# Twenty-four weight slots instead of twenty-two, four experts of layer 0 with fixed tiles, ranking beside the first tile, another order of tiles

## The chip, the cores and the metric

The kernel runs on one core of one Trainium2 chip. The metric is device time in microseconds (us) of one launch; less is better. Engines are named as in the profile: PE is TensorE, DVE is VectorE, ACT is ScalarE, POOL is GpSimd, and SP is SyncE, which here issues all transfers. PEld is the loading of PE's stationary operand, and a q behind an engine's name is its sequencer.

## The reference

A two-layer transformer over 256 latent and 256 context tokens, width 1024, in float32. Layer 0 mixes tokens with windowed attention and latent attention, layer 1 with differential attention. After each mixer stands a mixture of experts: every token picks one of 4 groups and in it 2 of 8 experts, 32 experts in all. Layer 0 routes 512 tokens (1024 assignments), layer 1 only the 256 latent ones (512).

```python
g_logits = h @ w_group + b_group                 # 4 groups
grp = argmax(g_logits); p_grp = softmax(g_logits)[grp]
e_logits = (h @ w_expert + b_expert)[grp]        # 8 experts of that group
top_p, top_i = top_k(softmax(e_logits), 2)
gate = p_grp * top_p / sum(top_p); eid = grp * 8 + top_i
y = sum over the 2 experts: gate * ((silu(x @ w1[e]) * (x @ w3[e])) @ w2[e])
x = x + mod * y
```

One expert has w1 and w3 of 1024 x 512 and w2 of 512 x 1024, 6 MB in float32. Both layers together read 64 experts, 384 half matrices of 1 MB.

## The kernel before

**Slots.** Weights and large activations live in one pool of `NS` = 22 slots of 128 partitions x 2048 floats (1 MB, line 48; the pool is made at line 123). `S` takes one, `free(n)` gives back n data slots and `freew(n)` n weight slots. All weight loads stand in one list in the order of use (`plan`); `pump` emits them, in the order of the program, while the weight slots in use are fewer than `NS - max(budget, data slots in use, ...)`. `budget(n)` sets how many slots are kept for data. A load waits on the chip until the last reader of its slot is done. SP issues them in list order.

**Experts.** For each layer the planner sorts experts by how many tokens they have, and rank decides the room: `_tiles` packs the rooms of ranks into tiles of 128 rows. Kind A is one expert of 128 rows, B two (96 and 32), C two of 64, D three (64, 32, 32), E four of 32. The first `NFIX[l]` experts are not ranked: they have 64 rows each and fixed tiles (called F below), so their weights can be loaded before routing is known. Before the change layer 0 has one such tile and then C E B C E A B C E D B C; layer 1 has two and then E C E B E C E C E. Both changed and unchanged orders have 13 tiles in layer 0.

A tile's loads, in order: w1 (two halves of each of its experts), w3, w2. So A has 6 loads, B and C 12, D 18, E 24. Per tile PE makes ffn1 for w1 (L1334), combines the tile before it (L1381), makes ffn1 for w3, transposes, then ffn2 with w2 (L1364). After each half of a product `freew` frees its slots. Behind every second tile (and behind the first) the tokens of the next pair of tiles are gathered (L1317).

**Ranking.** `rank(l)` (L1164, DVE) turns the counts into a permutation of ranks. `rank_ids` (L1187) makes expert numbers of it with two small matmuls (L1191) and two DVE copies (L1192, L1193), and lifts the limit: loads of ranked experts read their expert number into a register (L213), and `limits` holds `pump` back to the loads of fixed experts until then. `rank` runs in the last step of `ffn_in`; `rank_ids` stands in `group_gather(0)`, between the gather of the first tile (L1276, copies at L1302) and its transposes (L1308, copies at L1309), ahead of the first expert matmul.

**Around it.** Before the last tile `rest` (L1384) stands: a loop over blocks of 64 tokens of experts that have more tokens than room, behind a branch (L1394). `budget(4 - l + 2 nh)` rules the tiles: 8 in layer 0, 5 in layer 1; for the last two tiles it is 14 and 12. Ahead of tile 0 the budgets are 8 and 5 too.

Of the kernel before, what the change touches and what calls it, by code (L numbers as in the profile page):

```python
# [10 lines left out]
F32 = mybir.dt.float32  # L11
F32R = mybir.dt.float32r
BF = mybir.dt.bfloat16
# [6 lines left out]
P = 128  # L20
# [24 lines left out]
    CN[_n] = (_o, _o + _w)  # L45
    _o += _w
NCN = _o
NS = 22
KU = 2

ADL = 3
# [3 lines left out]

NFIX = (2, 4)


def _tiles(nf, rooms, order):

    fix = [[(r, 64), (r + 1, 64)] for r in range(0, nf, 2)]
    left = {}
    for n, r in enumerate(range(nf, NE)):
        left.setdefault(rooms[n] if n < len(rooms) else 32, []).append(r)

    kinds = {"A": (128,), "B": (96, 32), "C": (64, 64), "D": (64, 32, 32), "E": (32,) * 4}
    tiles = []
    for k in order:  # L70
        t = []
        for n, w in enumerate(kinds[k]):
            t.append((left[w].pop(0 if n % 2 == 0 else -1), w))
        tiles.append(t)
    assert not any(left.values())
    return fix + tiles


TILES = [_tiles(2, (128,) + (96,) * 3 + (64,) * 9, "CEBCEABCEDBC"), _tiles(4, (96,) + (64,) * 6, "ECEBECECE")]
NTS = [len(ts) for ts in TILES]  # L80
COLS = [[rw_ for t in ts for rw_ in t] for ts in TILES]
assert all(all(sum(w for _, w in t) == P for t in ts) for ts in TILES)
# [34 lines left out]
def model_kernel(ctx: ExitStack, tc: tile.TileContext, xin, small, cst, ada0, adaw, win, wuq, wukv, wout0, dwin,  # L117
                 wout1, ew, out):
    nc = tc.nc
    PE, ACT, DVE, GP, SP = nc.tensor, nc.scalar, nc.vector, nc.gpsimd, nc.sync  # L120
    PSUM = bass.MemoryType.PSUM
    cp = ctx.enter_context(tc.tile_pool(name="cp", bufs=1))
# [22 lines left out]
    def freew(n):  # L145
        st_["w"] -= n
        pump()
# [50 lines left out]
    cs = {}  # L198
# [77 lines left out]
    cnE = cp.tile([P, 2, NE], F32, name="cnE")  # L276
    ones2 = cp.tile([P, 2], F32, name="ones2")
    DVE.memset(ones2, 1.0 / D)
    onesM = cp.tile([P, P], F32, name="onesM")
    DVE.memset(onesM, 1.0)  # L280
    epst = cp.tile([P, 2], F32, name="epst")
    DVE.memset(epst[:, 0:1], EPS)
    DVE.memset(epst[:, 1:2], DEPS)
    identB = cp.tile([P, P], BF, name="identB")
    maskB = cp.tile([P, 2, P], BF, name="maskB")
    UB = cp.tile([P, P], BF, name="UB")
    onesB = cp.tile([P, P], BF, name="onesB")
    DVE.memset(onesB, 1.0)
# [755 lines left out]
    def ffn_in(h, torder):  # L1044
# [89 lines left out]
            for t in range(2):  # L1134
                h_lo(t, 0, ((GP, DVE))[t])
        yield
        if last:
            rank(l)
            yield

        TT(pe, e4, b8(m4), ALU.subtract)
        TT(gx, g, b4(gmax), ALU.subtract)
# [21 lines left out]
    def rank(l):  # L1164

        key, tmp, st = U((NE,)), U((NE,)), T((4,))
        kc, rk, cc = (st[0:64, n:n + 1] for n in range(3))
        key, tmp = key[0:64], tmp[0:64]
        perm, tm2 = U((64,)), U((NE,))[0:64]
        GP.memset(perm[0:64], 0.0)  # L1170
        DVE.scalar_tensor_tensor(out=key, in0=cnts[0:64], scalar=32.0, in1=byl("tie", l)[0:64], op0=ALU.mult, op1=ALU.add)
        TT(tmp, key, ident[0:64, 0:NE], ALU.mult)
        TT(tm2, key, ident[0:64, NE:64], ALU.mult)
        TT(tmp, tmp, tm2, ALU.add)
        RD(out=kc, in_=tmp, axis=AX.X, op=ALU.add)
        DVE.tensor_scalar(tmp, key, kc, None, op0=ALU.is_gt)
        RD(out=rk, in_=tmp, axis=AX.X, op=ALU.add)
        for q in range(2):
            r = slice(32 * q, 32 * q + 32)
            DVE.tensor_scalar(perm[r, r], byl("rkc", l)[r], rk[r], None, op0=ALU.is_equal)  # L1180
            if q == 0:
                DVE.tensor_scalar(cc, kc, byl("tiec", l)[0:64], 1.0 / 32, op0=ALU.subtract, op1=ALU.mult)
        perm_[0], perm_[1] = perm, cc
# [95 lines left out]
    def moe(l, T_, gens, pre=None, hook=None):  # L1279
# [1 line left out]
        nh = nt // SEQ  # L1281
        cs_ = lambda c: slice(c * P, (c + 1) * P)

        def group_gather(g, mid=None):

            xg = S((KC, 256))
            oh = oh_of(g, T_)
            n = P * len(GROUPS[l][g])
            if n == P:
                xts = []  # L1290
                pss = pre if g == 0 and pre else [psA(), psA()]
                if g == 0:
                    gather0(T_, (0, 1), pss, 4 if pre else 0)
                for hf in range(2):
                    ps = pss[hf]
                    if g:
                        for t in range(T_):
                            for a, src in enumerate((hi_c, lo_c)):
                                PE.matmul(ps, oh[:, t, 0:n], src(t, slice(hf * 512, (hf + 1) * 512)),
                                          start=(t == 0 and a == 0), stop=(t == T_ - 1 and a == 1))  # L1300
                    xts.append(U())
                    (ACT.copy, DVE.tensor_copy)[hf](xts[hf], ps)  # L1302
                if mid:
                    mid()
                for hf in range(2):
                    ps = psB()
                    for q in range(4):
                        PE.transpose(ps[:, cs_(q)], xts[hf][:, cs_(q)], ident)  # L1308
                    (ACT.copy, DVE.tensor_copy)[hf](xg.v[:, 4 * hf:4 * hf + 4, 0:n],  # L1309
                                                    ps.rearrange("p (c n) -> p c n", c=4))  # L1310
                return xg
            for c0 in range(0, KC, 2):
                ps = psB()
                for i in range(2):
                    for t in range(T_):
                        for a, src in enumerate((hi_c, lo_c)):
                            PE.matmul(ps[:, i * n:(i + 1) * n], src(t, cs_(c0 + i)), oh[:, t, 0:n],  # L1317
                                      start=(t == 0 and a == 0), stop=(t == T_ - 1 and a == 1))
                ACT.copy(xg.v[:, c0:c0 + 2, 0:n], ps[:, 0:2 * n].rearrange("p (c n) -> p c n", c=2))
            return xg  # L1320
# [6 lines left out]
                return wts[key].rearrange("p (k n) -> p k n", k=4)  # L1327
            return f

        def ffn1(ps, parts, m, xg, ns):  # L1330
            for hf in range(2):
                for k in range(4):
                    for sl, wt in parts:
                        PE.matmul(ps[sl, :], xg(hf * 4 + k, sl), wt(m, hf)[:, k, :], start=(hf == 0 and k == 0),  # L1334
                                  stop=(hf == 1 and k == 3))
                freew(ns)

        def hmid_of(hm, p1, p3, sl=None):
            sl = U() if sl is None else sl
# [128 lines left out]
            free(4)  # L1468

        pend = None  # L1470
        xg_g = group_gather(0, rank_ids)
        for gen in gens:
            for _ in gen:
                pass
# [2 lines left out]
        for p in range(NT):  # L1477
# [16 lines left out]
            pm = []  # L1494
            for m in range(2):
                pm.append(psA())
                ffn1(pm[m], parts, m, xgc, len(segs))
                if m == 0:
                    sl = U()
                    ACT.activation(sl, pm[0], AF.Silu)  # L1500
                else:
                    hm = U()
                    TT(hm, sl, pm[1], ALU.mult)  # L1503
                if pend is not None:
                    combine(m, pend[0][m], pend[1], range(2 if m and p == NT - 1 else 4))
                elif p == 0 and m == 0:
                    pt = permute_t(T_)
                elif p == 0:
                    permute(T_, pt)
# [76 lines left out]
    fill(3)  # L1586
    next(last)
    fill(KC - ADL - 3)
    next(last)
    finish = moe(0, 4, (last, gen), pre, fill_all)  # L1590


# [235 lines left out]
    budget(5)  # L1828
    last = ffn_in(half, [0, 1])
    fillq.extend([(1, -5, k) for k in range(4)])  # L1830
    for n in (0, 0, 4, 0, 0):
        next(last)
        fill(n)
    finish = moe(1, 2, (last,), None, fill_all)
# [156 lines left out]
```

## Time and profile before

| | us |
|---|---|
| median of 3 runs | 1509.83 |
| lowest and highest | 1509.78, 1511.85 |
| profiled execution | 1511.53 |
| its span, first to last instruction | 1509.6 |

| engine | busy us | share of the span |
|---|---|---|
| PE | 1308.4 | 87% |
| PEld | 720.0 | 48% |
| DVE | 609.6 | 40% |
| ACT | 381.8 | 25% |
| POOL | 125.8 | 8% |

All transfers together are 487.07 MB, 323 GB/s over the span. A share over the whole span mixes stages: two attention blocks and two expert phases follow each other, and each has its own limit. The table to read is therefore one of stages, and then the waits in each.

### The profile page before, as it was taken

The page shows a single profiled execution, that of the slowest core. Times are in us where ns is not written, and L with a number is a line of the kernel's source. Part 1 is how long each engine was busy: PE and PEld are TensorE (multiplying, and loading weights), DVE is VectorE, ACT ScalarE, POOL GpSimd, SP SyncE. Part 2 cuts the span into 40 slices and gives each one's busy share as a digit, 9 for nine tenths or more (in the row PEclk, how much of TensorE's full clock was granted, in tenths as well). Part 3 has the DMA queues.
Part 4 walks back from the last instruction along what each step waited for, and adds up shares of the span by engine and source line. Part 5 has one row for each costly group of instructions (what it writes and reads, how often), then busy time and mean ns, then how long its engine had stood idle before and what let it go on. Part 6 is the DMA issues. An engine that isn't in the chain of part 4 may idle for free. (4 is left out here: it accounts for less than half of the span.)

```text
span 1509.6 us, 21525 instructions
## 1 busy us (share of the span) xinstructions
PE 1308.4 (87%) x8297; PEld 720.0 (48%) x8297; DVE 609.6 (40%) x1495; ACT 381.8 (25%) x814; POOL 125.8 (8%) x109
## 2 busy tenths in 40 slices
PE   6996989989999789987998999887998786887865
PEld 4673668945435235422435897584432221323322
DVE  4588895464222222221328657945311110111113
ACT  4445655331111001110115434642110100101002
POOL 1134011210000000000004211311000000000000
PEclk9998999999999999999999999999999999999997
DMA  9525624379999999999996227466999999999993
GB/s 381 214 97 197 222 91 162 140 296 388 402 420 421 421 421 413 383 395 422 420 419 273 84 84 294 156 236 283 420 421 421 421 421 420 421 420 422 419 408 154
DMA packets 68635, 487.07 MB, mean 323 GB/s; under 512 B 7472, under 2 KB 7600, under 8 KB 10928
## 3 DMA queue, kind: packets, MB, share of 16 engines
q1 hardware_dynamic: 68528, 485.64, 79.2%
q8 instruction: 67, 1.10, 0.3%
q14 instruction: 40, 0.33, 0.1%
HBM read 484.57 MB, written 1.05 MB: 322 GB/s over the span
## 5 line engine op out<-in xcount | busy, mean ns | idle before, releaser
L1334 PE MATMUL psA<-s 128*32 128x512 f32 (+2 forms) x2336 | 418.8, 618 | 90.0 <-DMA s<-in_ew_dram 84.7
L1334 PEld LDWEIGHTS psA<-s 128*32 128x32 f32 (+2 forms) x2336 | 113.4, 121 | 374.4 <-issue 203.7
L1364 PE MATMUL psA<-s,u 128*32 128x512 f32 (+1 forms) x1168 | 194.6, 610 | 25.9 <-DMA s<-in_ew_dram 24.6
L1374 DVE SCALAR_TENSOR_TENSOR s<-psB,modT,s 128x256 f32<-128x256 f32 x296 | 120.4, 476 | 215.4 <-PE psB L1381 215.2
L1369 DVE SCALAR_TENSOR_TENSOR u<-psA,t,u 128x512 fp32r<-128x512 f32 x48 | 36.0, 751 | 250.0 <-ACT u L1368 250.0
L1364 PEld LDWEIGHTS psA<-s,u 128*32 128x32 f32 (+1 forms) x1168 | 55.3, 120 | 144.3 <-issue 94.6
L1503 DVE TENSOR_TENSOR u<-u,psA 128x512 f32<-128x512 f32 x24 | 16.5, 688 | 232.4 <-PE psA L1334 232.4
L1381 PE MATMUL psB<-u 128*128 128x512 f32 (+1 forms) x384 | 95.6, 370 | 12.6 <-DVE s L1374 8.8
L1358 ACT COPY u<-psB 128x512 f32<-128x512 f32 x24 | 14.1, 586 | 340.1 <-PE psB L1356 340.1
L394 PE MATMUL psB<-s 128*128 128x256 f32 (+1 forms) x296 | 96.2, 325 | 4.0 <-DVE s L887 4.0
L395 PE MATMUL psB<-s 128*128 128x256 f32 (+1 forms) x296 | 95.2, 322 | 0.4 <-DVE s L387 0.4
L396 PE MATMUL psB<-s 128*128 128x256 f32 (+1 forms) x296 | 95.1, 321 | 0.0
L1381 PEld LDWEIGHTS psB<-u 128*128 128x128 f32 x384 | 58.8, 189 | 71.0 <-issue 37.7
L1368 ACT ACTIVATE u<-psA,t 128x512 fp32r<-128x512 f32 x48 | 33.0, 687 | 196.9 <-PE psA L1364 194.4
L1500 ACT ACTIVATE u<-psA 128x512 f32<-128x512 f32 x24 | 14.3, 598 | 223.2 <-PE psA L1334 223.2
L1317 PE MATMUL psB<-s 128*128 128x256 f32 x544 | 68.0, 285 | 0.7 <-ACT u L1358 0.7
L387 DVE TENSOR_TENSOR s<-s 128x1024 fp32r<-128x1024 f32 (+3 forms) x56 | 51.3, 962 | 39.1 <-ACT s L384 39.1
L1317 PEld LDWEIGHTS psB<-s 128*128 128x128 f32 x544 | 65.8, 191 | 2.6 <-issue 1.6
L394 PEld LDWEIGHTS psB<-s 128*128 128x128 f32 x296 | 56.5, 191 | 13.9 <-DVE s L887 4.8
L394 PE MATMUL psA<-s 128*128 128x256 f32 (+1 forms) x208 | 62.4, 300 | 0.0
L395 PE MATMUL psA<-s 128*128 128x256 f32 (+1 forms) x208 | 60.5, 291 | 0.0
L396 PE MATMUL psA<-s 128*128 128x256 f32 (+1 forms) x208 | 60.5, 291 | 0.0
(350 smaller groups left out, 1726.4 us busy)
## 6 DMA issues: line engine op xcount, KB each, us to landing
s<-in_ew_dram SPq DMA_DIRECT2D x384, 1024.0 KB, 19.8
s<-in_adaw_dram SPq DMA_DIRECT2D x40, 1024.0 KB, 7.4
s<-in_dwin_dram SPq DMA_DIRECT2D x12, 1024.0 KB, 5.0
s<-in_ada_dram SPq DMA_DIRECT2D x8, 1024.0 KB, 19.9
s<-in_wout_dram SPq DMA_DIRECT2D x8, 1024.0 KB, 9.4
s<-in_win_dram SPq DMA_DIRECT2D x5, 1024.0 KB, 19.2
s<-in_xin_dram SPq DMA_DIRECT2D x2, 1024.0 KB, 8.9
s<-in_wuq_dram SPq DMA_DIRECT2D x1, 1024.0 KB, 19.2
```

The source lines that it names most:

```text
L387: eng.tensor_tensor(lo, src, hi.bitcast(F32), ALU.subtract)
L394: PE.matmul(ps, lh, rh, start=(k == 0), stop=False)
L395: PE.matmul(ps, lh, rl, start=False, stop=False)
L396: PE.matmul(ps, ll, rh, start=False, stop=(k == n - 1))
L1317: PE.matmul(ps[:, i * n:(i + 1) * n], src(t, cs_(c0 + i)), oh[:, t, 0:n], start=(t == 0 and a == 0), stop=(t == T_ - 1 and a == 1))
L1334: PE.matmul(ps[sl, :], xg(hf * 4 + k, sl), wt(m, hf)[:, k, :], start=(hf == 0 and k == 0), stop=(hf == 1 and k == 3))
L1364: PE.matmul(ps[sl, :], ht[:, k, sl], wt(2, hf)[:, k, :], start=(k == 0), stop=(k == 3))
L1368: ACT.activation(yh, ps, AF.Copy, scale=gsl)
L1369: DVE.scalar_tensor_tensor(out=yl, in0=ps, scalar=gsl, in1=yh.bitcast(F32), op0=ALU.mult, op1=ALU.subtract)
L1374: DVE.scalar_tensor_tensor(out=xc(c)[:, HALF[s]], in0=ps[:, HALF[s]], scalar=modT[:, l, 5, c, s:s + 1], in1=xc(c)[:, HALF[s]], op0=ALU.mul ...
L1381: PE.matmul(ps[:, 0:nt], ysp[a][:, cs_(q)], oht[:, 0:nt], start=(a == 0), stop=(a == 1))
L1503: TT(hm, sl, pm[1], ALU.mult)
```

## The change

- `NS` is 24. The room comes from three places: `onesM` (a 128 x 128 float tile of ones) becomes a one-column tile that is broadcast when read; the bf16 masks and identity (`maskB`, `identB`) lie in the unused tail of the slot that holds the constants; and the reserve for software-made DMA descriptors is set to 1024 bytes of a partition.
- `NFIX[0]` is 4. Layer 0 has the tiles F F E B A C E B C D B C E instead of F C E B C E A B C E D B C. Seven ranks have 64 rows instead of nine. Layer 1's tiles stay.
- `rank(l)` is called after `group_gather(0)`, and `rank_ids` by `ffn1` of tile 0 between its two halves of w1.
- The copies in the gather of a single tile are all ACT's; half of them were DVE's.

```diff
-NS = 22
+NS = 24
-NFIX = (2, 4)
+NFIX = (4, 4)
-TILES = [_tiles(2, (128,) + (96,) * 3 + (64,) * 9, "CEBCEABCEDBC"), _tiles(4, (96,) + (64,) * 6, "ECEBECECE")]
+TILES = [_tiles(4, (128,) + (96,) * 3 + (64,) * 7, "EBACEBCDBCE"), _tiles(4, (96,) + (64,) * 6, "ECEBECECE")]
...
-    onesM = cp.tile([P, P], F32, name="onesM")
-    DVE.memset(onesM, 1.0)
+    ones1 = cp.tile([P, 1], F32, name="ones1")
+    DVE.memset(ones1, 1.0)
+    onesM = ones1.to_broadcast([P, P])
...
-    identB = cp.tile([P, P], BF, name="identB")
-    maskB = cp.tile([P, 2, P], BF, name="maskB")
+    csb = cs[0][:, NCN:NCN + 192].bitcast(BF)
+    maskB, identB = csb[:, 0:256].rearrange("p (a n) -> p a n", a=2), csb[:, 256:384]
...
         yield
-        if last:
-            rank(l)
-            yield
...
-        def group_gather(g, mid=None):
+        def group_gather(g):
...
-                    (ACT.copy, DVE.tensor_copy)[hf](xts[hf], ps)
-                if mid:
-                    mid()
+                    ACT.copy(xts[hf], ps)
...
-                    (ACT.copy, DVE.tensor_copy)[hf](xg.v[:, 4 * hf:4 * hf + 4, 0:n],
-                                                    ps.rearrange("p (c n) -> p c n", c=4))
+                    ACT.copy(xg.v[:, 4 * hf:4 * hf + 4, 0:n], ps.rearrange("p (c n) -> p c n", c=4))
...
-        def ffn1(ps, parts, m, xg, ns):
+        def ffn1(ps, parts, m, xg, ns, mid=None):
...
                 freew(ns)
+                if mid and hf == 0:
+                    mid()
...
-        xg_g = group_gather(0, rank_ids)
+        xg_g = group_gather(0)
+        rank(l)
...
-                ffn1(pm[m], parts, m, xgc, len(segs))
+                ffn1(pm[m], parts, m, xgc, len(segs), rank_ids if p == m == 0 else None)
...
     fill(KC - ADL - 3)
-    next(last)
     finish = moe(0, 4, (last, gen), pre, fill_all)
...
-    for n in (0, 0, 4, 0, 0):
+    for n in (0, 0, 4, 0):
...
-    nc = bacc.Bacc("TRN2", target_bir_lowering=False, num_devices=1)
+    nc = bacc.Bacc("TRN2", target_bir_lowering=False, num_devices=1, dynamic_dma_scratch_size=1024)
```

## Rows read from the trace of the kernel before

**Rows 1.** The page: what the DMA engines moved, in 40 slices of 37.7 us.

```profile
GB/s 381 214 97 197 222 91 162 140 296 388 402 420 421 421 421 413 383 395 422 420 419 273 84 84 294 156 236 283 420 421 421 421 421 420 421 420 422 419 408 154
```

**Rows 2.** Stages: length, busy (count) PE, PEld, DVE, ACT, POOL; PEclk, DMA, GB/s.

```profile
320.90:785.80 464.90, 421.33 (x2592) 184.51 (x2594) 132.09 (x371) 57.14 (x92) 0.00 (x0) 0.99 0.99 409
785.80:1039.60 253.80, 230.40 (x1580) 186.92 (x1576) 174.15 (x360) 116.72 (x253) 57.36 (x54) 0.97 0.52 201
1039.60:1485.40 445.80, 360.40 (x2024) 130.45 (x2024) 74.84 (x217) 45.37 (x78) 0.00 (x0) 0.97 0.99 412
```

**Rows 3.** Waits of PE, 1039.6 to 1486, then 786 to 1039: total, times, longest.

```profile
PE psA L1334 <- DMA s<-in_ew_dram: 61.2, 51, 1.5
...
PE psB L1744 <- DVE u L1737: 8.9, 10, 4.8
```

**Rows 4.** Stretches with low traffic and one without, columns as in rows 2.

```profile
316.40:323.30 6.90, 6.66 (x36) 4.10 (x34) 4.72 (x23) 3.30 (x5) 0.00 (x0) 0.91 0.17 45
323.30:400.00 76.70, 72.79 (x412) 31.84 (x408) 29.65 (x113) 11.27 (x18) 0.00 (x0) 1.00 0.97 392
546.80:645.60 98.80, 96.92 (x549) 48.99 (x548) 28.53 (x70) 14.12 (x23) 0.00 (x0) 1.00 0.96 393
638.60:644.60 6.00, 6.00 (x29) 2.06 (x30) 0.75 (x1) 1.27 (x2) 0.00 (x0) 1.00 0.24 74
1035.70:1045.60 9.90, 9.66 (x45) 4.54 (x46) 5.55 (x28) 2.72 (x4) 0.00 (x0) 0.89 0.11 28
1060.00:1480.00 420.00, 338.59 (x1926) 122.86 (x1922) 67.99 (x186) 40.84 (x71) 0.00 (x0) 0.97 1.01 420
```

**Rows 5.** Waits of SP, around 320, 640, 1040, 760 and 1440.

```profile
SPq L213 <- DVE cnE L1193: 10.5, 1, 10.5
...
SPq L165 <- PE psA L1364: 17.1, 2, 14.7
...
SPq L165 <- PE psA L1334: 17.4, 1, 17.4
...
SPq L1394 <- SPq L1394: 14.2, 4, 11.1
...
SPq L1394 <- SPq L1394: 14.5, 2, 14.0
```

**Rows 6.** Expert loads issued 236 to 320.5 and 945 to 1043: count, size, landing.

```profile
s<-in_ew_dram SPq DMA_DIRECT2D x12, 1024.0 KB, 4.8
...
s<-in_ew_dram SPq DMA_DIRECT2D x17, 1024.0 KB, 6.4
```

**Rows 7.** Instructions in order of time, 318.9 to 321: start us, us, engine, line.

```profile
319.04 0.40 PE L1191 MATMUL psB<-u,sm 32*128 32x32 f32 x2
...
319.14 0.69 DVE L1302 COPY u<-psA 128x512 f32<-128x512 f32 x1 [0.33 <-PE psA L1276]
...
319.59 1.09 PE L1308 MATMUL psB<-identR,u 128*128 128x128 f32 x8
...
320.92 0.65 PE L1334 MATMUL psA<-s 128*64 128x512 f32 x2 [0.24 <-ACT s L1309]
```

**Rows 8.** Layer 0's last expert load, then each layer's last product (PE).

```profile
L165 SPq DMA_DIRECT2D s<-in_ew_dram x1: 333/333/333, 773.0 to 773.0; - x1
...
DMA to landing us min/median/max: 12.8/12.8/12.8
...
784.94 7.09 PE L1364 MATMUL psA<-s,u 128*64 128x512 f32 x32
...
1485.49 5.02 PE L1364 MATMUL psA<-s,u 128*32 128x512 f32 x26 [1.40 <-DMA s<-in_ew_dram]
```

**Rows 9.** End of gate arithmetic (DVE), start of tile 0 last product (PE).

```profile
329.19 0.22 DVE L1160 TENSOR_TENSOR PG<-u 128x64 f32<-128x64 f32 x1
...
339.43 4.94 PE L1364 MATMUL psA<-s,u 128*64 128x512 f32 x22
```

**Rows 10.** The kernel's last 14.4 us, columns as in rows 2.

```profile
1495.20:1509.60 14.40, 5.35 (x23) 4.77 (x23) 6.50 (x18) 4.50 (x8) 0.00 (x0) 0.50 0.18 73
```

## The prediction

> **What bounds the kernel now.** I read the traffic line of the page first [rows 1]: three high stretches, the first 38 us at 381 GB/s and the two expert phases near 420, with valleys where the two attention blocks run. The stage table puts bounds on it [rows 2]. From the first expert matmul of layer 0 (320.9) to the landing of its last expert matrix (785.8) the DMA share is 0.99 at 409 GB/s; the same phase of layer 1, 1039.6 to 1485.4, shows 0.99 at 412. Between them the share is 0.52 and TensorE is busy 230.4 of 253.8 us. So two stages are bound by the weight stream and the rest by the compute chain. The wait table agrees [rows 3]: in layer 1's phase TensorE's longest wait is for expert loads (61.2 us in 51 waits), in the attention between the phases its longest is for VectorE, and no wait for a load stands near the top.
>
> A stage bound by a stream ends at the moment when the stream became continuous, plus the loads still to come, plus the holes in it, plus the compute behind the last load. An expert phase is 192 loads of 1024 KB; at the 420 GB/s of 1060 to 1480 [rows 4] one takes 1.0486 MB / 420 GB/s = 2.50 us. So I look for holes and for their causes.
>
> **Holes** [rows 4]. At 316.4 to 323.3 the rate is 45 GB/s, at 638.6 to 644.6 it is 74, at 1035.7 to 1045.6 it is 28. In lost time: 6.9 x (1 - 45/420) = 6.2 us, 6.0 x (1 - 74/420) = 4.9 us, 9.9 x (1 - 28/420) = 9.2 us. From 323.3 to 400 the rate is 392, which is 76.7 x (1 - 392/420) = 5.1 us more, spread out. The queue's own waits name the causes [rows 5]. The first hole is SyncE waiting 10.5 us for the expert numbers (L1193): only the 12 loads of the fixed tile may go out before the ranking, and exactly 12 did [rows 6]. The second is a wait of 14.7 us for a slot that L1364 had not yet freed: from 546.8 to 645.6, tiles A, B and C, TensorE is busy 96.9 of 98.8 us while these tiles need only 30 loads, 75 us, so the stream ran ahead until all 22 - 8 = 14 weight slots were full. The third is a wait of 17.4 us for the first release by L1334: 17 loads had gone out [rows 6], which is 22 less the budget of 5.
>
> **The change, part by part.**
>
> *Two more slots, layer 1.* Every bound in `pump` is NS minus a budget, so each rises by 2: 19 loads ahead instead of 17, below the limit of 24. The two added loads move into the idle valley, and the load that waits for the first release is number 20, not 18. 2 x 2.50 = 5.0 us off the 9.2 us hole. Bounds: 0 if the slots are not filled in time, 9.2 if the hole goes altogether.
>
> *Two more slots and four fixed experts, layer 0.* Before tile 0 the bound is 24 - 8 = 16 loads, and with 24 fixed ones the limit no longer cuts it. It looks like a gain of four loads (16 instead of 12), but before the change two loads went out at 321 without any release, so in the first tiles load n+2 of the new kernel waits for the release that load n waited for before: 2 x 2.50 = 5.0 us. Tiles 0 and 1 are bound by TensorE, so the rest of the first hole turns into idle time behind releases there. Bounds: 0, and 6.2 + 5.1 = 11.3 if hole and shortfall before 400 both go.
>
> *Order of tiles.* Old: F C E B C E A B C E D B C. New: F F E B A C E B C D B C E (F fixed, two experts; A one expert, 6 loads; B and C two; D three; E four, 24 loads). In the new order A stands between B and C right after an E. There the stream starts with no lead, and B, A, C need 75 us of it against at most the same 98.8 us: a lead of at most 24 us, 9.5 loads, below 16 slots. Then comes an E with 60 us of loads, which uses it up. So the hole at 638.6 has no successor: 4.9 us. Bounds: below nothing, if another place gets such a hole (-4.9), to +4.9; I take the upper end since the slots exceed the lead.
>
> *Last tile of layer 0: E instead of C.* Now the last load is issued at 773.0 and lands 12.8 us later, at 785.8, while TensorE does the last product from 784.94 to 792.03 without waiting for it [rows 8]: it ends 6.2 us behind the stream. Layer 1 ends with an E: its last product goes on at 1485.49, when the last load is there, and takes 5.02 us [rows 8]. 6.2 - 5.0 = 1.2 us. Bounds: 1.2, and -3.4 if the SyncE stop at the overflow branch (L1394, 11.1 us of waiting before the last tile [rows 5]) leaves a hole, now that no lead covers it; layer 1 has the same stop before its E (14.0 us, [rows 5]), inside the stretch that keeps 420 GB/s [rows 4], so I take 1.2.
>
> *Ranking moved.* The two small matmuls of `rank_ids` (319.04 to 319.59, [rows 7]) leave the path between gather and first expert matmul: 0.55 us. Against it, the second gather copy, now by VectorE beside ScalarE's (0.69 us), is queued behind the first one on ScalarE. Net 0.4 us per layer, from -0.6 to +0.55: 0.8 us for both. `rank` itself is VectorE work that ran beside the gather matmuls and stays there.
>
> *Costed at nothing.* `rank_ids` now stands between the first and second half of tile 0's first product: 0.55 us more inside a tile whose releases come in bursts, while two loads are under way each time. Its copies of the expert numbers queue on VectorE behind the gate arithmetic, which ends at 329.4 (L1160); what waits for them is the 25th load of the layer, and that also needs the ninth release, in the product that starts at 339.43 [rows 9]: 10 us of cover, and 1 us lost for each us beyond it. The masks in the tail of the constants' slot, the one-column `onesM` and the smaller scratch move no work; there are few readers of each, and I allow 1 us either way for them together. The attention stages have no wait for loads to gain from.
>
> **Sum.** 5.0 + 5.0 + 4.9 + 1.2 + 0.8 = 16.9 us. The rows are of an execution of 1511.5 us, whose span is 1509.6 and 1.9 lies around it; the median of the runs is 1509.83. What goes is inside the span, so I take it off the median: 1509.8 - 16.9 = 1492.9 us.
>
> **Rivals.**
> *The order gives nothing.* Another tile fills the slots, or the stop before the E costs what its tail gives. Then 4.9 + 1.2 are missing: 1499.0. For it: the lead is worked out with the tile lengths of the old order, and slots are freed in bursts; against it, 9.5 loads of lead is far from 16.
> *The early shortfall goes too.* If the 5.1 us before 400 come from the hole ahead of them and not from releases: 1487.8.
> *Cold TensorE.* After its last E tile the kernel ran 14.4 us at a granted clock of 0.50, 1.2 GHz [rows 10]. With an E now ending layer 0, the combine and the start of layer 1's norm could run so: dense work of 14.4 us at that clock would take 7.2 at full, so 1500.1. Against it: the E tiles inside the phases are followed by dense tiles, and the mean clock there is 0.97 to 0.99 [rows 2]. The Trainium skill (TensorE: Matmul & The Clock Gate, section on HAM oscillation) says that an array which waits for DMA between bursts is put back on the slow clock. By that rule alone this rival would be the forecast, but in the rows the starved phases stay near full speed.
> *The slots are not filled.* If data tiles hold the two slots, or SyncE's order keeps the loads back: 1492.9 + 10.0 = 1502.9, or no change at all if the order fails too.
> *Overflow: slower.* Fixed experts have 64 places each, whatever their count; an expert over its room goes through the loop in `rest`, which reads 6 more matrices per 64 tokens: at least 6 x 2.50 = 15 us, and about 15 + 98.8/3 = 48 if a tile's compute (a third of the stretch 546.8 to 645.6) stands in series with it. One such block at over 20 us makes the kernel slower than before, e.g. 1492.9 + 30 = 1523. The reference's own routing says no: experts 0 to 3 of layer 0 get 9, 35, 29 and 30 assignments, and the 12th largest of the others, the first with a room of 32, gets exactly 32.
>
> **Chances.** Forecast 0.57; order gives nothing 0.20; shortfall goes too 0.08; cold TensorE 0.06; slots not filled 0.04, half of it without any change; overflow 0.05, a fifth of it within 0.2%. A difference under 0.2% (3 us) can't be told from no change. So faster 0.57 + 0.20 + 0.08 + 0.06 + 0.02 = 0.93, same 0.03, slower 0.04. The range goes from 1486 (shortfall gone and small gains) to 1501.5 (order without effect, or cold TensorE, and 1 us of small costs).
>
> **What would show it.** Right: 16 loads before tile 0 and 19 before layer 1's first expert matmul; the wait for L1193 gone; the layer 1 hole down to about 4 us; no stretch below 400 GB/s from 400 to the last load of layer 0; layer 0's last landing near 770 and each stage after it as long as now. Wrong: a new SyncE wait for L1364 in the middle of layer 0, a hole before its last tile, or 0.50 clock after it.

## The result, and the profile after

| | before | after |
|---|---|---|
| median, us | 1510.62 (4 runs) | 1493.82 (4 runs) |
| lowest and highest | 1509.78, 1511.85 | 1492.70, 1494.84 |
| profiled execution, its span | 1511.53, 1509.6 | 1494.84, 1493.1 |

The ratio is 0.9888, with a 95% interval of 0.9871 to 0.9905: 16.8 us less (14.4 to 19.5), where the prediction said 16.9 (1492.9 us). With an interval that wide, the agreement to 0.1 us is luck.

To see where the time went, cut the span at four events of the trace: the first expert matmul of layer 0 (E1), the landing of the last expert load of layer 0, the first expert matmul of layer 1 (E2), and the last landing of layer 1. Between E1 and the landing, and between E2 and the landing, lie the two streams of 192 loads.

| us | to E1 | stream 0 | to E2 | stream 1 | end | span |
|---|---|---|---|---|---|---|
| before | 320.9 | 464.9 | 253.8 | 445.8 | 24.1 | 1509.6 |
| after | 319.0 | 454.6 | 254.3 | 440.3 | 24.8 | 1493.1 |
| difference | -1.9 | -10.3 | +0.5 | -5.5 | +0.7 | -16.5 |
| the prediction's terms | -0.4 | -9.9 | -1.6 | -5.0 | 0 | -16.9 |

(The terms: 0.4 of ranking in each layer; two slots 5.0 and order 4.9 in stream 0; last tile 1.2 ahead of E2; two slots 5.0 in stream 1.)

The page's traffic line of after, 40 slices of 37.3 us, beside [rows 1]: the slices with 383 and 395 in the middle of layer 0 are gone.

```profile
GB/s 380 284 94 169 254 77 178 123 307 373 415 421 420 422 421 421 420 421 421 406 421 285 85 85 303 155 232 289 422 421 421 421 421 421 422 421 421 419 415 141
```

The stages and the stretches of after, columns as in [rows 2] (busy and count of PE, PEld, DVE, ACT, POOL; then PEclk, DMA share, GB/s). The first three answer [rows 2], the others [rows 4]:

```profile
319.00:773.60 454.60, 422.06 (x2599) 186.59 (x2598) 132.27 (x371) 58.42 (x94) 0.00 (x0) 0.99 0.99 409
773.60:1027.90 254.30, 230.13 (x1572) 186.35 (x1572) 173.49 (x357) 116.23 (x252) 57.82 (x54) 0.95 0.55 208
1027.90:1468.20 440.30, 369.00 (x2029) 131.57 (x2028) 74.26 (x216) 46.00 (x79) 0.00 (x0) 0.93 1.00 413
...
320.10:327.00 6.90, 6.90 (x34) 2.29 (x30) 4.87 (x30) 1.51 (x4) 0.00 (x0) 1.00 0.46 164
327.00:400.00 73.00, 70.76 (x423) 32.08 (x421) 27.49 (x94) 10.86 (x17) 0.00 (x0) 1.00 0.96 387
400.00:773.60 373.60, 343.30 (x2140) 151.74 (x2140) 99.91 (x248) 45.08 (x73) 0.00 (x0) 0.98 1.01 419
624.00:664.00 40.00, 33.71 (x234) 11.09 (x226) 10.45 (x25) 3.15 (x5) 0.00 (x0) 0.96 1.01 421
1024.00:1033.90 9.90, 9.66 (x45) 4.92 (x45) 4.69 (x29) 3.79 (x6) 0.00 (x0) 0.88 0.11 31
1040.00:1460.00 420.00, 352.79 (x1958) 126.61 (x1958) 70.40 (x195) 41.05 (x72) 0.00 (x0) 0.93 1.01 420
```

Two things are to be seen. From 400 to the last load of layer 0 no hole like that of before is left (419 GB/s). One dent remains, ahead of the last tile, where SP stands at the overflow branch (L1392):

```profile
720.00:740.00 20.00, 16.52 (x98) 5.08 (x96) 3.25 (x7) 1.98 (x3) 0.00 (x0) 1.00 0.96 393
```

It loses 20 x (1 - 393/420) = 1.3 us, so the sign "no stretch below 400 GB/s" failed by a little. And the hole at the start of layer 1 has not shrunk at all: 31 GB/s over 9.9 us, where [rows 4] had 28 over 9.9 us. Yet the stream behind it ends 5.5 us sooner.

SP's waits in after, the first row around 320, the second around 1030, the third from 600 to 773, beside [rows 5]:

```profile
SPq L165 <- PE psB L1190: 9.5, 2, 9.4
...
SPq L165 <- PE psB L1190: 17.2, 2, 17.0
...
SPq L1392 <- SPq L1392: 13.8, 7, 2.5
```

Expert loads of after that were issued ahead of layer 0's and of layer 1's tile 0 (count, size, median us to landing), beside [rows 6]:

```profile
s<-in_ew_dram SPq DMA_DIRECT2D x16, 1024.0 KB, 5.5
...
s<-in_ew_dram SPq DMA_DIRECT2D x19, 1024.0 KB, 6.9
```

The wait for the expert numbers (10.5 us) is gone, and so is the wait for a slot in the middle of layer 0 (14.7 us). The wait for the first release of layer 1 is as long as before, 17.0 us against 17.4; the profile names L1190 as its end, the small ranking matmuls, which now stand right behind the first half of tile 0's first product. The counts are the forecast ones.

### The profile page after: what moved, and what is told of

Same layout as the page of the kernel before. It is cut to its first block, busy times and chain, and to the rows that moved or that the text cites. A ratio compares the mean times of both kernels' runs of the same rounds, so it can differ in the third digit from the quotient of the medians.

```text
span 1493.1 us, 21498 instructions
## 1 busy us (share of the span) xinstructions
PE 1313.9 (88%) x8297; PEld 721.4 (48%) x8297; DVE 607.3 (41%) x1491; ACT 383.8 (26%) x818; POOL 126.6 (8%) x109
## 5 line engine op out<-in xcount | busy, mean ns | idle before, releaser
L1330 PE MATMUL psA<-s 128*32 128x512 f32 (+2 forms) x2336 | 424.9, 635 | 71.5 <-DMA s<-in_ew_dram 65.7
L1502 DVE TENSOR_TENSOR u<-u,psA 128x512 f32<-128x512 f32 x24 | 16.5, 688 | 229.3 <-PE psA L1330 229.3
L1499 ACT ACTIVATE u<-psA 128x512 f32<-128x512 f32 x24 | 14.4, 599 | 212.9 <-PE psA L1330 212.9
## 6 DMA issues: line engine op xcount, KB each, us to landing
s<-in_ew_dram SPq DMA_DIRECT2D x384, 1024.0 KB, 19.7
s<-in_adaw_dram SPq DMA_DIRECT2D x40, 1024.0 KB, 7.4
s<-in_dwin_dram SPq DMA_DIRECT2D x12, 1024.0 KB, 8.3
s<-in_ada_dram SPq DMA_DIRECT2D x8, 1024.0 KB, 19.9
s<-in_wout_dram SPq DMA_DIRECT2D x8, 1024.0 KB, 7.5
s<-in_win_dram SPq DMA_DIRECT2D x5, 1024.0 KB, 19.9
s<-in_xin_dram SPq DMA_DIRECT2D x2, 1024.0 KB, 8.6
s<-in_wuq_dram SPq DMA_DIRECT2D x1, 1024.0 KB, 20.8
```

## The experiments

Each is compared with the kernel before, run on the same chip. The medians of before on these chips were 1508.5 to 1508.7 us, with single runs from 1502.5 to 1514.5. Each edit is against before or against after, as its title says. The stages of their profiles, cut as above:

| us | to E1 | stream 0 | to E2 | stream 1 | end | ratio of medians (95%) |
|---|---|---|---|---|---|---|
| before | 320.9 | 464.9 | 253.8 | 445.8 | 24.1 | 1 |
| x8 memory only | 320.8 | 462.2 | 256.2 | 447.3 | 22.5 | 0.9995 (0.998, 1.001) |
| x3 fixed only | 319.9 | 458.8 | 253.1 | 445.8 | 24.0 | 0.9992 (0.9975, 1.0008) |
| x2 fixed and order | 321.4 | 458.2 | 257.1 | 446.6 | 25.5 | 0.9987 (0.9974, 1.0001) |
| x1 slots only | 319.4 | 455.4 | 255.8 | 440.4 | 22.5 | 0.9923 (0.9906, 0.9940) |
| x6 after, 23 slots | 317.7 | 456.6 | 257.7 | 443.6 | 25.9 | 0.9952 (0.9932, 0.9971) |
| x12 after, two slots held in layer 1 | 319.1 | 455.0 | 255.7 | 445.4 | 22.7 | 0.9955 (0.9938, 0.9972) |
| x5 after, old order | 319.4 | 455.4 | 255.0 | 442.7 | 24.8 | 0.9918 (0.9901, 0.9936) |
| x4 after, old ranking place | 317.6 | 455.0 | 254.9 | 440.4 | 25.1 | 0.9917 (0.9895, 0.9938) |
| x7 after, C last | 316.6 | 455.7 | 253.6 | 441.2 | 22.7 | 0.9908 (0.9893, 0.9923) |
| x10 after, budget 7 ahead | 316.2 | 456.4 | 254.4 | 440.8 | 25.3 | 0.9925 (0.9905, 0.9945) |
| x11 after, budgets + 2 | 317.7 | 455.9 | 256.0 | 441.5 | 24.8 | 0.9919 (0.9907, 0.9932) |
| x9 after again | 317.6 | 455.2 | 255.9 | 441.7 | 22.4 | 0.9891 (0.9866, 0.9916) |
| after | 319.0 | 454.6 | 254.3 | 440.3 | 24.8 | 0.9888 (0.9871, 0.9905) |

Read the columns before the ratios. The streams fall into groups that follow the number of slots; the other three columns scatter by 2 to 5 us between executions, the kernel after included.

### Slots alone (x1, on before)

```diff
-NS = 22
+NS = 24
+ the memory edits (ones1, masks in the constants' tail, scratch 1024)
```

> The kernel before with 24 slots and the memory edits that make room for them; order, fixed experts and ranking as before. Terms that add up (the prediction's sum): 5.0 us in each layer, so 1510.6 - 10.0 = 1500.6. Rival, overlap: the hole in the middle of layer 0's stream came when 14 slots were full, so 16 slots shorten it by 2 x 2.5 us as well, and the 4.9 us booked for the order belong to the slots just as much: 1510.6 - 14.9 = 1495.7.

Measured: 1496.88 us, ratio 0.9923, so -11.6 us; the span of its profile, 1493.5, is that of after within 0.4. Stream 1 has the forecast gain (440.4). Stream 0 gained 9.5 us against before, not 5.0, with the old order and only 12 loads ahead of tile 0. The stretch E1+305 to E1+345, in which before has its middle hole, in x1, x8 and x3; and for each the 10 us from E1+214 (columns as in [rows 2]):

```profile
624.40:664.40 40.00, 38.80 (x280) 18.39 (x279) 11.27 (x27) 6.18 (x10) 0.00 (x0) 1.00 1.00 411
533.40:543.40 10.00, 9.68 (x36) 3.22 (x37) 0.75 (x1) 0.69 (x1) 0.00 (x0) 0.79 1.01 419
```
```profile
625.80:665.80 40.00, 37.81 (x263) 18.87 (x261) 10.85 (x27) 6.08 (x10) 0.00 (x0) 1.00 0.89 367
534.80:544.80 10.00, 8.18 (x30) 1.90 (x31) 0.00 (x0) 0.58 (x1) 0.00 (x0) 0.66 1.01 419
```
```profile
624.90:664.90 40.00, 37.10 (x258) 17.66 (x261) 10.52 (x26) 5.49 (x9) 0.00 (x0) 0.99 0.97 400
533.90:543.90 10.00, 8.35 (x37) 2.85 (x38) 0.75 (x1) 0.69 (x1) 0.00 (x0) 1.00 1.01 419
```

With 24 slots and the old order the rate is 411 GB/s there: hole nearly closed, 40 x (1 - 411/420) = 0.9 us lost, where x8, with 22, loses 40 x (1 - 367/420) = 5.0. So with 24 slots the hole closes without the new order, as the overlap theory says. The medians do not decide between the theories: the interval of x1, -14.2 to -9.1 us, takes in the -10.0 of the terms that add up and just leaves out the -14.9 of overlap.

### Order and fixed tiles at 22 slots (x2, x3, on before)

```diff
-NFIX = (2, 4)
+NFIX = (4, 4)
-TILES = [_tiles(2, (128,) + (96,) * 3 + (64,) * 9, "CEBCEABCEDBC"), ...
+TILES = [_tiles(4, (128,) + (96,) * 3 + (64,) * 7, "EBACEBCDBCE"), ...     (x2)
+TILES = [_tiles(4, (128,) + (96,) * 3 + (64,) * 7, "EBCEABCEDBC"), ...     (x3)
```

> The kernel before with four fixed experts and the new order of tiles in layer 0; 22 slots, ranking as before. Prediction's sum: 4.9 for the hole and 1.2 for the tail, 1510.6 - 6.1 = 1504.5. Rival: the first hole, behind the limit of 12 loads, is worth its own length, and lifting it to the 14 loads that the slots allow gives 2 x 2.5 us more: 1499.5.

> The kernel before with four fixed experts, and the second fixed tile in the place of the first C tile of the old order; 22 slots. Prediction: nothing, 1510.6, since in tiles 0 and 1 each load waits for the same release as before. Rival: the two loads that may now go out before the ranking come off the stream, 1510.6 - 5.0 = 1505.6.

Measured: x2 1506.86 us (-1.9, interval -3.9 to +0.2), x3 1507.76 (-1.2, -3.8 to +1.2). So x2 leaves out both the -6.1 of the prediction's terms and the -11.1 of the rival; x3 takes in the forecast 0 and leaves out the rival's -5.0. The same stretch in x2:

```profile
626.40:666.40 40.00, 34.50 (x256) 12.29 (x258) 11.21 (x26) 3.83 (x6) 0.00 (x0) 1.00 1.01 421
```

The new order does close the hole with 22 slots: 421 GB/s, and loads 135 to 139 (counted from 0) land in 9.9 us, where before took 14.8 and x8 15.5. So the mechanism of the prediction is there; but little of it reaches the median. In x2's profile stream 0 is 4.0 to 6.7 us shorter than in x8 and before, and 0.9 to 3.3 of that goes again between the streams. x3, with the old order, has 12.1 us at that place, although no edit touches it, and its stream 0 is only 0.6 us longer than x2's. These two traces (of runs of 1510.4 and 1504.5 us, beside medians of 1506.9 and 1507.8) do not show that the order shortens the stream. The rows of x3 above show what differs: x8 ran the end of the E tile ahead of A, B and C at a mean clock of 0.66 (E1+214 to E1+224), x3 at 1.00. Before was as slow as x8 there, in the same stretch:

```profile
534.90:544.90 10.00, 6.73 (x28) 1.44 (x29) 0.60 (x1) 0.00 (x0) 0.00 (x0) 0.73 1.02 422
```

Tile A started at E1+225.9 in before, 223.3 in x8 and 220.2 in x3, so the full slots waited longer in the first two. What the clock is worth there shows in the last part of that E tile, the 26 matmuls behind its last load, in before, x3 and x1 (start, us):

```profile
540.26 6.59 PE L1364 MATMUL psA<-s,u 128*32 128x512 f32 x26 [1.44 <-DMA s<-in_ew_dram]
...
536.59 3.62 PE L1364 MATMUL psA<-s,u 128*32 128x512 f32 x26 [1.44 <-DMA s<-in_ew_dram]
...
533.72 5.54 PE L1366 MATMUL psA<-s,u 128*32 128x512 f32 x26 [0.58 <-DMA s<-in_ew_dram]
```

The mean clock over them is 0.54 in before, 1.00 in x3 and 0.64 in x1. So x3's 2.2 us over 9.9 are what is left of the hole at the full clock. x1 was delayed by 1.9 us, and had no hole (9.9 us for loads 135 to 139): with 24 slots a delay of that size did not reach the stream.

### Old order with the rest of after (x5, on after)

```diff
-TILES = [_tiles(4, (128,) + (96,) * 3 + (64,) * 7, "EBACEBCDBCE"), ...
+TILES = [_tiles(4, (128,) + (96,) * 3 + (64,) * 7, "EBCEABCEDBC"), ...
```

> The changed kernel with the old order of tiles in layer 0 (the first C is the second fixed tile). Terms that add up: the hole of 4.9 us comes back and the tail of 1.2: 1493.8 + 6.1 = 1499.9. Rival, overlap: with 16 slots the stream doesn't run out of slots in that stretch, the hole stays away, and only the tail is lost: 1493.8 + 1.0 = 1494.8.

Measured: 1496.22 us, ratio 0.9918. Stream 0 is 455.4 us, 0.2 and 0.8 more than in the two traces of after. The hole does not come back: loads 135 to 139 land in 9.9 us. The ratio is 0.0030 +- 0.0024 over that of after, 4.5 us (0.8 to 8.2), which takes in the 6.1 of the terms that add up as well as the 1.0 of overlap; x10 below says what such a difference is worth. The stream, with its 0.8 at most, speaks for overlap.

### 23 slots, and after again (x6, x9, on after)

```diff
-NS = 24
+NS = 23
```

> The kernel after with 23 slots: one load fewer ahead of each expert phase (15 before tile 0 of layer 0, 18 before layer 1). Theory A, a slot is worth one load time per stream-bound phase, and the new order is hole-free with 15 slots too: each of the two phases ends 2.50 us later against its first expert matmul (layer 0: 457.1 instead of 454.6 us to the last landing; layer 1: 442.8 instead of 440.3), total +5.0 us on the kernel after, ratio of the two 1.0033. Theory B, a threshold: the 24th slot is what closes the hole in the middle of layer 0, and what it adds beyond is small: either the hole comes back (a step of over 4 us between loads 135 and 139, +8 us or more) or 23 slots already suffice (+1 us or less in layer 0, +2.5 in layer 1).

> The changed kernel itself, unaltered, on this chip, to compare the other three with. Both theories: the two expert phases come out as in the first trace of it (454.6 and 440.3 us from first expert matmul to last landing, within 1 us), since they are set by the stream; the attention stage may come out 1 to 4 us longer or shorter, with the stretches at the granted clock of 0.50. If instead the phases move by more than 2 us between two executions of one kernel, the stage differences read so far are not due to the edits.

Measured: x6 1501.50 us, x9 1492.82 (its runs from 1488.45 to 1497.82). The streams of x9 are 0.6 and 1.4 us longer than in the first trace of after: the kernel's own scatter, and in layer 1 more than the 1 us that was expected. With 23 slots layer 1 takes 443.6 us, 2.4 over the mean of the eight traces with 24 (441.1), and 2.6 under the mean of the five with 22 (446.2, x12 among them). So layer 1 goes in equal steps, 446.2, 443.6, 441.1, the middle one from a single trace. Layer 0 takes 456.6 us, 1.4 to 2.0 over after, and no hole comes back; since the nine traces with 24 slots there reach from 454.6 to 456.4, one slot in layer 0 is not clear of the scatter. The streams explain 3.2 us of the 8.6 by which the two spans differ; the end (25.9 against 22.4) and the stage ahead of E2 (257.7 against 255.9) make most of the rest, and both scatter by 2.4 to 2.9 us among the kernels with 24 slots (22.4 to 25.3 and 253.6 to 256.0), though x6 lies 0.6 and 1.7 beyond. The ratios differ by 0.0061 +- 0.0032, 9.2 +- 4.8 us, which just takes in the forecast 5.0.

### The memory edits alone (x8, on before)

```diff
-    onesM = cp.tile([P, P], F32, name="onesM")
+    onesM = ones1.to_broadcast([P, P])
+    csb = cs[0][:, NCN:NCN + 192].bitcast(BF)
+    maskB, identB = ...
+ dynamic_dma_scratch_size=1024
```

> The kernel before with the three memory edits alone (one-column onesM, masks and identity in the tail of the constants, descriptor reserve of 1024 bytes), still 22 slots. My theory, costed at nothing: ratio 1.000, within 1 us, all stages as in the kernel before (464.9 and 445.8 us for the two expert phases). Rival: the edits themselves carry a part of the gain (fewer memsets and copies at the start, where the first expert matmul came 1.9 us sooner): -1 to -2 us, all of it before the first expert matmul.

Measured: 1508.52 us, ratio 0.9995. E1 comes at 320.8, as in before: the 1.9 us that E1 gained in after is not theirs. The middle hole recurs; of stream 0's 2.7 us less, the landings show 2.9 at loads 32 to 35, where before had one longer step, and the rest moves back and forth. Costing these edits at nothing was right, within the interval (-3.0 to +1.5 us).

### Ranking in its old place (x4, on after)

```diff
+        if last:
+            rank(l)
+            yield
...
-        xg_g = group_gather(0)
-        rank(l)
+        xg_g = group_gather(0, rank_ids)
...
-                ffn1(pm[m], parts, m, xgc, len(segs), rank_ids if p == m == 0 else None)
+                ffn1(pm[m], parts, m, xgc, len(segs))
```

> The kernel after with ranking in its old place (rank in the last step of ffn_in, rank_ids between gather and transposes, gather copies shared by ScalarE and VectorE). My theory from the prediction: 0.4 us longer per layer between the first gather matmul and the first expert matmul, so +0.8 us, with the loads ahead of tile 0 (16 and 19) and the two streams as they are. Rival from the traces so far (the handover was only 0.27 us shorter in the kernel after): +0.3 us per layer or less. Rival the other way: with the expert numbers known before the first expert matmul, the loads behind them are issued sooner and the hole ahead of tile 0's releases shrinks: faster than the kernel after by 1 to 5 us.

Measured: 1495.91 us against 1492.82 of x9 on the same chip; the ratios differ by 0.0026 +- 0.0033. The handover tells more than the median. PE's instructions in order of time ahead of layer 0's first expert matmul (start us, us, engine, line; the last row of each is E1), first x4, then after:

```profile
314.64 0.86 PE L1278 MATMUL psA<-s 128*128 128x512 f32 x3
315.67 0.40 PE L1193 MATMUL psB<-u,sm 32*128 32x32 f32 x2 [0.17 <-DVE u L1182]
315.91 0.38 PE L1193 MATMUL psB<-u,t 32*128 32x32 f32 x2
316.22 1.20 PE L1310 MATMUL psB<-identR,u 128*128 128x128 f32 x8
317.55 0.65 PE L1336 MATMUL psA<-s 128*64 128x512 f32 x2
```
```profile
315.86 1.84 PE L1275 MATMUL psA<-s 128*128 128x512 f32 x6
...
317.53 0.60 PE L1305 MATMUL psB<-identR,u 128*128 128x128 f32 x4
...
318.43 0.66 PE L1305 MATMUL psB<-identR,u 128*128 128x128 f32 x4 [0.29 <-ACT u L1301]
...
319.01 0.65 PE L1330 MATMUL psA<-s 128*64 128x512 f32 x2
```

From the end of the gather to E1, x4 takes 317.55 - 315.50 = 2.05 us, after 319.01 - 317.70 = 1.31. In layer 1 it is 1.82 against 1.26, and before has 1.8 in both. So the new place is worth 0.5 to 0.7 us per layer, a little over the 0.4 of the forecast. The rival that loads come sooner with the old place falls: stream 0 is 455.0.

### C as layer 0's last tile (x7, on after)

```diff
-... "EBACEBCDBCE"), ...
+... "EBACEBCDBEC"), ...
```

> The kernel after with its last two tiles exchanged, E C instead of C E, so that layer 0 ends with the two-expert tile as before the change. The prediction's term: layer 0's last product ends 6.2 us behind the last landing instead of 5.0, +1.2 us. Rival from the traces so far (kernels with 24 slots that end with C show 4.9 to 5.0 us there): 0, or 0.4 us sooner than with E. Rival cold TensorE: with C last the half-clock stretch behind layer 0's end is shorter and the attention 1 to 4 us shorter than the 248.9 and 250.7 us of the kernel after.

Measured: 1494.25 us, ratio 0.9908. The last product of layer 0 in x7, in x8 (C last too, 22 slots) and the last part of it in after (E last); PE in order of time, start and us:

```profile
770.06 7.09 PE L1362 MATMUL psA<-s,u 128*64 128x512 f32 x32
```
```profile
780.84 7.09 PE L1366 MATMUL psA<-s,u 128*64 128x512 f32 x32
```
```profile
773.69 5.37 PE L1362 MATMUL psA<-s,u 128*32 128x512 f32 x26 [0.57 <-DMA s<-in_ew_dram]
```

x7 ends at 777.15, 4.8 us behind its last landing (772.31); x8 ends 5.0 behind its own (782.96); after ends 5.4 behind. The tail does not hang on the last tile, and the 6.2 us of [rows 8] was one execution's. From the last landing to E2 the six kernels with C last take 253.1 to 256.2 us, mean 254.6, the eight with E last 254.3 to 257.7, mean 255.7. If ending with an E costs anything, it is about 1 us, and the two ranges overlap too far to show it.

### Two attempts that took no slot away (x10, x11, on after)

```diff
-    budget(5)                      (ahead of tile 0 of layer 1: both)
+    budget(7)
-        budget(4 - l + 2 * nh)     (x11 only)
+        budget(4 + l + 2 * nh)
-                budget(10 + 2 * nh)
+                budget(10 + 2 * l + 2 * nh)
```

> The kernel after, but ahead of tile 0 of layer 1 the budget is 7 instead of 5: 17 loads go out before the first expert matmul, the 18th and 19th only at it, still without waiting for any release. From tile 0 on all 24 slots are used. Theory A, the gain of a slot is that one load of the phase needs no release, wherever in the idle stretch it is moved: the two loads (2 x 2.50 us) fit into the hole of 11.4 us behind the last early load, the load behind them still waits for the first release of tile 0, and layer 1's phase stays at 440.3 to 441.7 us from first expert matmul to last landing; total within 1 us of the kernel after. Theory B, what counts is that the loads are done before the first expert matmul, as the prediction put it for layer 1 (17 loads ahead instead of 19): +5.0 us, phase 445.3.

> The kernel after, but with all budgets of layer 1's expert phase raised by 2, so that this phase has 22 slots as before; layer 0 keeps 24. Theory A, each phase gains its own 2 x 2.50 us from the slots: layer 1's phase comes back to 445.8 us (as in the kernel before), everything ahead of it stays, total +5.0 to +5.5 us on the kernel after. Rival: the slots' worth lies in layer 0 and the hole there; layer 1's 5.4 us in the traces came from something else that changed (the clock, the ranking): within 2 us of the kernel after.

Measured: 1497.87 and 1496.80 us; stream 1 takes 440.8 and 441.5 us. The edits did not do what I meant. Expert loads of layer 1 that were issued ahead of its tile 0, x10 and then x11:

```profile
s<-in_ew_dram SPq DMA_DIRECT2D x19, 1024.0 KB, 6.9
```
```profile
s<-in_ew_dram SPq DMA_DIRECT2D x19, 1024.0 KB, 6.9
```

A budget counts in the order of the program, but the pool still has 24 buffers. The load that is written down at a later release finds one that nobody reads any more, so SP issues it without waiting. Neither run says anything on layer 1's slots; x12 was made for it. The issue times agree: from the 20th load on, 3.7 us behind E2, they are those of after. The two have another use: with the loads of after their ratios lie 0.0037 and 0.0031 over its 0.9888. By these 5.6 and 4.7 us two slots would seem to be gone, and the counts and the streams say that they are not. Differences of this size between builds, as x4, x5 and x7 show them, can therefore not be put down to their edits; where they come from is open.

### Two slots held in layer 1 (x12, on after)

```diff
+    held = [S((2048,)), S((2048,))]
+    for b in held:
+        GP.memset(b.t[:, 0:1], 0.0)
-    budget(5)
+    budget(7)
... the two budgets of the phase as in x11
     finish = moe(1, 2, (last,), None, fill_all)
+    for b in held:
+        GP.tensor_copy(T((1,)), b.t[:, 0:1])
+    free(2)
```

> The kernel after, but two of the 24 slots are really taken away from layer 1's expert phase: two data tiles are taken ahead of ffn_in of layer 1, one column of each is written by GpSimd and read again only behind the phase, and the budgets of the phase are raised by 2 with them. (In the two runs before, a higher budget alone left all 24 buffers in turn, and the queue issued the same 19 loads ahead.) Theory A, each phase gains its own 2 x 2.50 us from two more buffers: 17 loads ahead of tile 0, the 18th waits for the first release, layer 1's phase at 445.8 us from first expert matmul to last landing instead of 440.3 to 441.7, and the total +5 us on the kernel after, all of it in layer 1's phase. Rival: layer 1's 5 us had another cause (clock, ranking): phase within 2 us of 441.

Measured: 1500.87 us, ratio 0.9955. Loads ahead of tile 0 of layer 1, SP's wait for the first release, the hole (E2-3.9 to E2+6.0, as 1024.0:1033.9 of after) and the stream:

```profile
s<-in_ew_dram SPq DMA_DIRECT2D x17, 1024.0 KB, 6.8
```
```profile
SPq L165 <- PE psB L1190: 17.6, 2, 17.4
```
```profile
1025.80:1035.70 9.90, 9.90 (x44) 5.18 (x44) 4.34 (x27) 3.89 (x6) 0.00 (x0) 0.81 0.11 29
1029.70:1475.10 445.40, 367.50 (x2029) 130.95 (x2028) 74.22 (x216) 46.01 (x79) 0.31 (x2) 0.95 1.00 413
```

Stream 1 is back at 445.4 us (before: 445.8) with everything ahead of it as in after, at the same rate of 413 GB/s and with the same hole. The new ranking is still in place here, and gives none of it; nor does the clock, for x11 has 0.96 and 441.5 us. So layer 1's gain is two loads of 2.5 us that need no release. The median says more than that: the ratio is 0.0067 over that of after, 10 us where 5 were expected, while the spans of the two profiles differ by 4.8. The other 5 are of the size that x10 and x11 show with all slots in use.

## Why the prediction was right, and where its steps were not

**Layer 1's slots: size right, place wrong.** 5.0 forecast, 5.5 in the pair of traces, 5.1 between the means of 22 and 24 slots, and x12 gives it back. But the prediction took the 5.0 "off the 9.2 us hole" and expected a hole of about 4. The hole is as long as ever: the last four loads ahead of it are issued as slots come free at the end of `ffn_in`, 19 to 13 us ahead of E2 in both kernels, and the next one 3.7 us behind E2, at tile 0's first release. The two added loads go out earlier in the valley. What shrinks is the number of loads behind the hole, 173 instead of 175. The formula stands (start of the continuous stream, plus loads to come); I should have put the 2 x 2.50 into its second term.

**Layer 0's slots and order: sum nearly right, parts counted twice.** 5.0 + 4.9 = 9.9 forecast, 10.3 in the pair (7.1 to 8.9 from the mean of before and x8, 463.5, to the nine traces with 24 slots there, 454.6 to 456.4). The step that failed is the addition. x1 is 6.8 us shorter than x8 and 9.5 shorter than before from slots alone, and x5, with the old order, is within 0.8 of after. One hole was there to be closed, and either edit closes it (9.9 us for loads 135 to 139 in x1, x5 and x2). Ahead of it the slots brought about 3 us, not 5.0: load 134 lands at E1+314.6 to E1+317.8 with 22 slots, at E1+311.5 to E1+313.3 with 24; why not the whole 5.0 is open. With the order in place, slots give the same 3 (x2's 458.2 to 454.6 and 455.2). A forecast made from x1 would read: slots first, 7 to 9; order on top, under 1. What the order gives at 22 slots is not shown: x2's stream is 4.0 to 6.7 us shorter than that of x8 and before, but x3's, with the old order, is 3.4 to 6.1 shorter. And the pair's 10.3 is luck in part. The hole's 4.9 us were, by x3, 2.2 at the full clock; and 3.0 us arose in before alone, where loads 31 to 35 took 13.4 us, against 10.4 in x8 and 10.7 in x3.

**Fixed tiles.** That four more early loads bring no more than slots do was right: x1 with 12 loads ahead has the stream of after with 16. Its load 23 lands 5.9 us later against E1 than that of after, its load 47 only 0.6.

**Last tile.** The term of 1.2 us was a misreading of two single rows: 7.09 us from 784.94 against 5.02 from 1485.49 [rows 8]. PE does not wait for the last load of a C (x7, x8 and [rows 8]), so its tail hangs on where PE is then: 4.8 to 6.2 us in the six traces with C last, with a mean of 5.2. With E last it is 3.7 to 6.6 in eight, with a mean of 5.3.

**Ranking.** 0.8 us forecast for both layers, 0.5 to 0.7 per layer in the handovers. The wait behind DVE cost nothing: no wait for L213 is left.

**What the sum left out.** E1 came 1.9 us sooner, of which the handover explains 0.5. Most of the rest goes with the clock: with PE's instructions of the two traces lined up, 1.1 us arise between 24 and 30 us. The 16 us from 20 to 36, far ahead of any expert, in before, in after and in x3, which ranks in the old place:

```profile
20.00:36.00 16.00, 13.22 (x106) 7.53 (x98) 8.91 (x27) 4.81 (x11) 2.11 (x1) 0.79 1.01 421
```
```profile
20.00:36.00 16.00, 13.20 (x107) 8.24 (x100) 9.95 (x30) 5.77 (x14) 1.97 (x1) 0.89 1.01 421
```
```profile
20.00:36.00 16.00, 13.21 (x110) 7.82 (x110) 9.73 (x30) 5.29 (x13) 2.42 (x2) 0.89 1.02 421
```

The three traces with 0.79 there (before, x8 and x2) reach E1 at 320.8 to 321.4; x3, with neither the memory edits nor the new ranking, reaches it at 319.9. x9, the same kernel as after, has E1 1.4 us sooner still, and again the clock differs: from 215 to 240 it is 1.00 in x9 and 0.93 in after. The stage ahead of E2 was forecast 1.6 us shorter and came out 0.5 longer, the end 0.7 longer. In the order of the table the errors are -1.5, -0.4, +2.1, -0.5 and +0.7 us: they add up to +0.4, and that they cancel is luck, to the extent of some 2 us.

**The rivals.** "The order gives nothing" is true of the order beside 24 slots, but its time (1499.0) does not come, since the slots close the hole. "The early shortfall goes too" did not happen: 387 GB/s from 327 to 400 against 392. "Slots not filled" is refuted by the counts of 16 and 19. "Overflow" never showed: SP's longest stop at L1392 from 600 to 773 is 2.5 us. "Cold TensorE" would have cost 7.2 us behind layer 0; the means with E last and with C last differ by 1.2 us (x7). Its sign did show, though: in the 29.4 us behind the last landing the mean clock is 0.82 to 0.86 in the eight traces with E last and 0.88 to 0.94 in the six with C last. In before and then in after:

```profile
785.80:815.20 29.40, 25.51 (x131) 12.57 (x128) 19.02 (x45) 16.02 (x37) 11.52 (x14) 0.94 0.99 409
```
```profile
773.60:803.00 29.40, 24.96 (x122) 11.63 (x123) 17.94 (x41) 14.10 (x34) 10.89 (x13) 0.82 1.02 422
```

So the sign came and the price did not: 1.2 us lie within the scatter, far from 7.2. The Trainium skill (TensorE: Matmul & The Clock Gate, section on HAM oscillation) says that waits for DMA between bursts put TensorE back on the slow clock; the stage table of after does show 0.93 in layer 1, where before had 0.97, but the stream there still runs at 413 GB/s, so the clock costs that stage nothing.

**What stays open.** Whether the 0.0035, 5 us, between the ratios of x1 (0.9923) and after (0.9888) are real, and how they divide: the stages show 1.1 to 1.3 us of ranking and at most 0.8 of stream, and builds with the same loads differ by up to 0.0037.

## What to carry to other kernels

In a stage that a stream bounds, a buffer more can be worth one load time (2.5 us each in layer 1; in layer 0 two gave about 3, beside the hole), for it is one load fewer behind the point where loads begin to wait for releases; look for it there and not in the length of the hole. Before adding the gains of two edits, ask whether both close the same hole: here either did, and the second edit found almost nothing left to close. Where a forecast rests on single rows of stages that no edit touches, look at the scatter between executions first.

## What the hardware showed that was not expected

The stages that compute binds are not of one length. From the last landing of layer 0 to E2, the 14 traces with a profile span 253.1 to 257.7 us, and what goes with it, on the whole, is the granted clock. That stage in x8, whose edits lie far from it, as a row beside [rows 2]:

```profile
783.00:1039.10 256.10, 232.99 (x1574) 189.83 (x1570) 173.77 (x359) 116.74 (x253) 57.44 (x54) 0.95 0.52 200
```

It took 253.1 and 253.8 us in the two traces with a mean of 0.97, 253.6 to 256.2 at 0.95 or 0.96, and 257.1 and 257.7 at 0.94: over 4 us from one end to the other. It is not the clock alone: x1 and x7 both have 0.96 and lie 2.2 us apart. The size of the middle hole went with the clock as well: before and x8, which ran the end of the E tile ahead of A, B and C partly at 1.2 GHz (0.50), lost 4.9 and 5.6 us at loads 135 to 139, x3 at the full clock 2.2. With 22 slots a hole of the stream can thus be in part a matter of PE's clock. With 24 slots, delays of 1.9 us (x1) and 2.1 (x5) left no hole; no trace shows a longer one.
